# Another order of the three float32r products of a two-bank matmul group

## The chip, the cores and the metric

The kernel runs on one core of a Trainium2 chip. The metric is the time of one execution on the device in microseconds (us); three runs of the kernel before gave 841.36, 841.49 and 846.52, a median of 841.49. The profile is of one execution. Its engines are TensorE (PE for the matmuls, PEld for the loads of their weights), VectorE (DVE), ScalarE (ACT), GpSimd (POOL) and SyncE (SP, which issues most DMAs).

## The reference

One inference step of a two-layer decoder trunk, for 512 prompt rows and 8 sample rows (520 rows) of 1,024 channels, all in float32:

```python
# layer 0
z = x @ w_in                                   # 1024 -> 7 x 1024
a_val, a_gate, b_post, c_pre, h, g = split(z)  # g has 2 x 1024
a = silu(layer_norm(causal_conv31(a_val * sigmoid(a_gate))))
b = b_post * causal_conv3(c_pre * h)
x = layer_norm(alpha * x + (concat(a, b) * silu(g)) @ w_out)
# layer 1
z = x @ w_in_c                                 # 1024 -> 3 x 2048
u, v, g = split(z)
v = layer_norm(gelu(v))
y = gelu(u) * (tril(w_s) v + b_s) * silu(g)    # chunks of 128 positions, 8 heads
x = layer_norm(alpha * x + y @ w_out_c)
```

It returns the rows of both groups, the last rows of the conv inputs and the v rows of the sample group.

## The kernel before

**Tiling.** Channels lie on the 128 partitions and the 520 rows on the free dimension, so that x is 8 k tiles of 128 x 520. A weight *unit* is a block of 1,024 input channels by 128 output channels: 8 tiles (one for each k tile) of 128 x 128. One unit gives one output tile z of 128 x 520, which fills two PSUM banks with 260 rows each (`TH = 260`; `hs(h)` is the h-th half of the rows).

**Three products.** To keep float32's precision with float32r operands, both operands are split into a high and a low part. `load_unit` (L115 to L125) does so for the weights: SyncE's queue loads `raw`, ScalarE copies it to `whi` (L121), and VectorE or GpSimd subtracts to get `wlo` (L124; `ON_POOL` says which units are GpSimd's). The rows have parts named xh and xl, x1h and x1l, or yh and yl, of which the first is the high one. Each product is then hi x high + lo x high + hi x low, so that a unit takes 8 k tiles x 3 products x 2 halves = 48 matmuls of 128 x 128 weights and 260 columns.

**The three places that write such products.** `mm2` (L152 to L163, matmul at L157) does a whole unit into two banks; it serves the gate, val, c, h and post projections, both silu gates (z_gb, z_ga), the first half of each output projection (z_o, z_q), ten of the v units, and u and the gate of layer 1 (z_u, z_gc). `mm` (L136 to L146, matmul at L141) does one half of the rows into one bank; it serves the second halves of the output projections (z_p) and six of the v units. The first two units (z_first, matmul at L207) are done as their data arrives, in a loop of their own: within a k tile, for each of the three products, for each of the two units, both halves.

**Buffers.** The split weights rotate through 12 buffers, hi and lo in turn (some units use others), and `unit` asks for a unit five calls ahead (`LEAD = 5`). The `raw` buffers are three. The tiles z of two banks rotate through two, so that a call of mm2 may run while the tile before is read. VectorE and ScalarE read both halves of z in one instruction, but for the last gate of each branch (two silu steps, L415), z_o's third tile (two adds, L461) and the first units.

**Order.** The program is written in its logical order and a planner orders each engine's queue by a simulated timeline, with the order of writing as the priority. The wide conv of layer 0 (`acc`, L269, 30 multiply-adds of 128 x 512 for each of 8 channel tiles on VectorE) is marked as background work: it fills VectorE between the steps that the projections need, among them `apad` (L306), `ch` (L325), the short conv `sB` (L332) and the product with z_post (L392). `split_y` (L395 to L405) makes the high and low parts of the gated rows; `out_part` (L473) does the second half of an output projection with its layer norm.

Of the kernel before, what the change touches and what calls it, by code (L numbers as in the profile page):

```python
# [17 lines left out]
D = 1024  # L18
# [12 lines left out]
ALPHA = 4.0 ** 0.25  # L31
EPS = 1e-5

# columns of the packed per-channel parameters
PA_W = 0
PA_B = 31
PA_G = 32
# [13 lines left out]
def decoder_kernel(  # L51
# [30 lines left out]
    def xs_slot(dt, name):  # L82
        return slots.tile([P, T], dt, tag="X", name=name, bufs=16)
# [16 lines left out]
    def mt(name):  # L100
        return mps.tile([P, 512], F32, tag="m", name=name)
# [7 lines left out]
    def hs(h):  # L109
        return slice(h * TH, (h + 1) * TH)  # L110

# [1 line left out]
    n_units = 2 + wu.shape[0]  # L113
    units = [None, None]

# [16 lines left out]
    def unit(n):  # L132
        while len(units) < min(n + 1 + LEAD, n_units):
            load_unit(("M", 4) if len(units) in EXTRA else ("W", 12))
        return units[n]
# [16 lines left out]
    def mm2(z, w, ah, al):  # L152
        hi, lo = w
        for k in range(KT):
            for h in range(2):
                for j, (a, b) in enumerate(((hi, ah), (lo, ah), (hi, al))):
                    nc.tensor.matmul(  # L157
                        z[h][:, :TH],
                        a[:, k, :],
                        b[k][:, hs(h)],  # L160
                        start=(k == 0 and j == 0),
                        stop=(k == KT - 1 and j == 2),
                    )  # L163

    # products of a constant until the first rows are there, so that the array's clock is up by then
    warm = const.tile([P, P], BF16, name="warm")
    nc.vector.memset(warm, 1.0)
    wps = mt("warm")
    for j in range(NWARM):
        nc.tensor.matmul(wps[:, :P], warm, warm, start=True, stop=True)  # L170

    # the input rows come with the first two weight units, one k tile after the other, and the
    # products follow in that order
    xh, xl = [], []
    w0h, w0l = [], []
    zg = zt("z_first")
# [2 lines left out]
    for k in range(KT):  # L179
# [5 lines left out]
        q, j = k // 4, k % 4  # L185
        nc.sync.dma_start(raw[:, j], w0[:, k])
        cuts = 2 if k == 0 else 1
# [3 lines left out]
        h = xs_slot(F32R, f"xh_{k}")  # L191
        lo = xs_slot(F32R, f"xl_{k}")
# [22 lines left out]
    load_unit()  # L215
    pa = const.tile([P, KT, NPA], F32, name="pa")
    nc.sync.dma_start(pa, pa_in)
    # powers of two, so float32r holds them as well
    ones_r = const.tile([P, P], F32R, name="ones_r")
    ones_d = ones_r.bitcast(F32)  # L220
    nc.gpsimd.memset(ones_d, 1.0 / D)
# [6 lines left out]
    neg_half = const.tile([P, NS], F32, name="neg_half")  # L228
    nc.gpsimd.memset(neg_half, -0.5)

    # ================= layer 0 =================
    unit(1)
    xs = []
    for j in range(2):
        t = wpool.tile([P, 4, NS, WA], F32, tag="M", name=f"xs_{j}", bufs=4)
# [46 lines left out]
    n = 0  # L282
    for i in range(KT):
# [44 lines left out]
        s = slots.tile([P, T], F32, tag="SB", name=f"sB_{i}", bufs=8)  # L328
# [9 lines left out]
                op1=ALU.add,  # L338
            )

    # the sample rows of both convolutions
    nc.gpsimd.dma_start(cbs_out, xb)
    prodb = btmp("prodb")[:, : KT * NS * WB].rearrange("p (a b c) -> p a b c", a=KT, b=NS)
    nc.vector.tensor_tensor(
# [23 lines left out]
                    cA[i][:, SEQ:], cas[:, i - 4 * j, :], AF.Identity, bias=pa[:, i, PA_B : PA_B + 1]  # L368
                )

    # layer norm of the wide convolution over the channels, then silu
    def mean_of(m, src, name):
        """the sum of src / D over the channels, from its two float32r parts"""
        both = tpool.tile([P, T], F32R, tag="B", name=f"parts_{name}", bufs=4)
        nn = src.shape[-1]
        hi, lo = both[:, :nn], both[:, TH : TH + nn]
        nc.scalar.copy(hi, src)
        nc.vector.tensor_tensor(lo, src, hi.bitcast(F32), op=ALU.subtract)
        nc.tensor.matmul(m, ones_r, hi, start=True, stop=False)
        nc.tensor.matmul(m, ones_r, lo, start=False, stop=True)  # L380
# [11 lines left out]
        nc.vector.tensor_tensor(two(sB[i]), zh(z), two(sB[i]), op=ALU.mult)  # L392

    def split_y(i, g, other, tag, parts):
        """y = g * other as its two parts, in that many cuts of the rows"""  # L395
        h = y_slot(F32R, f"yh_{tag}{i}")
        lo = y_slot(F32R, f"yl_{tag}{i}")
        for j in range(parts):
            c = slice(j * T // parts, (j + 1) * T // parts)
            nc.vector.tensor_tensor(g[:, c], g[:, c], other[:, c], op=ALU.mult)  # L400
            nc.scalar.copy(h[:, c], g[:, c])
            nc.vector.tensor_tensor(lo[:, c], g[:, c], h[:, c].bitcast(F32), op=ALU.subtract)
        yh.append(h)
        yl.append(lo)
# [66 lines left out]
    gated(cA, "a")  # L471

    def out_part(base, c0, c1, yh, yl, res, lnc, done, last=False, pool_sub=()):  # L473
        """The second half of an output projection for the rows c0..c1, the residual, and the layer
        norm over the channels. The sums of the norm are of the rows less the mean of their first
        512 channels, so that no large mean cancels in the variance."""
        c = slice(c0, c1)
        nn = c1 - c0
        key = f"{base}_{c0}"
# [92 lines left out]
    def split_x1(d, c0, c1):  # L572
# [10 lines left out]
    out_part(n, TH, T, yh, yl, res, LN0_G, split_x1)()  # L583
    n += KT

    # ================= layer 1 =================
    wt = wpool.tile([P, NH, P], F32, tag="M", name="wt", bufs=4)
    nc.gpsimd.dma_start(wt, wsT_in)
    bs = wpool.tile([P, NH, P], F32, tag="M", name="bs", bufs=4)
    nc.gpsimd.dma_start(bs, bs_in)  # L590
    # wt[s, h, t] is kept where s <= t
    nc.gpsimd.affine_select(
        wt, wt, pattern=[[0, NH], [1, P]], compare_op=ALU.is_ge, fill=0.0, base=0, channel_multiplier=-1
    )
    # and its float32r parts, for the column sums
    wth, wtl = [], []
    for j in range(2):
        w = wt[:, 4 * j : 4 * j + 4, :].rearrange("p a b -> p (a b)")
# [29 lines left out]
    for i in range(NVF):  # L628
        z = one(i, f"z_v{i}_1")[:, :TH]
        mm(z, unit(n + i), x1h, x1l, hs(1))  # L630
        t = vt[i]
# [18 lines left out]
    def v_finish():  # L650
        v_tok(NV - 1)
        for c in range(NC):
            nc.vector.bn_aggr(mv[:, c, :], stats[:, c, :, :].rearrange("p a b -> p (a b)"))
        nc.vector.tensor_scalar_add(rs, mv[:, :, 1], EPS)
        nc.gpsimd.tensor_tensor(rs, rs, neg_half[:, :NC], op=ALU.pow)
        for i in range(NV):
            for c in range(NC):
                nc.vector.tensor_scalar(
                    vtok[i][:, c * P : (c + 1) * P],
                    vtok[i][:, c * P : (c + 1) * P],  # L660
                    mv[:, c, 0:1],
                    rs[:, c : c + 1],
                    op0=ALU.subtract,
                    op1=ALU.mult,
                )
        # column sums of the causal weights, for the shift of the norm
        for j in range(2):
            m = mt(f"rows_{j}")
            nc.tensor.matmul(m, ones_r, wth[j], start=True, stop=False)
            nc.tensor.matmul(m, ones_r, wtl[j], start=False, stop=True)  # L670
            nc.scalar.mul(
                rowsum[:, 4 * j : 4 * j + 4, :].rearrange("p a b -> p (a b)"), m, float(D)
            )
        # the sample rows' layer norm
        ssum = tiny.tile([P, NS], F32, name="ssum")
        nc.vector.tensor_reduce(ssum, vs.rearrange("p a b -> p b a"), axis=AX.X, op=ALU.add)
        m = mt("vs_mean")
        nc.tensor.matmul(m[:, :NS], ones_d, ssum, start=True, stop=True)
        smean = tiny.tile([P, NS], F32, name="smean")
        nc.vector.tensor_scalar_mul(smean, m[:, :NS], 0.5)  # L680
        bc = lambda t: t[:, None, :].to_broadcast([P, NV, NS])
        nc.vector.tensor_tensor(vs, vs, bc(smean), op=ALU.subtract)
        vq = mixs
        nc.vector.tensor_tensor(vq, vs, vs, op=ALU.mult)
        qsum = tiny.tile([P, NS], F32, name="qsum")
        nc.vector.tensor_reduce(qsum, vq.rearrange("p a b -> p b a"), axis=AX.X, op=ALU.add)
        m = mt("vs_var")
        nc.tensor.matmul(m[:, :NS], ones_d, qsum, start=True, stop=True)
        srs = tiny.tile([P, NS], F32, name="srs")
        nc.vector.tensor_scalar(srs, m[:, :NS], 0.5, EPS, op0=ALU.mult, op1=ALU.add)  # L690
        nc.gpsimd.tensor_tensor(srs, srs, neg_half, op=ALU.pow)
        nc.vector.tensor_tensor(vs, vs, bc(srs), op=ALU.mult)
        pb = lambda j: pv[:, :, j : j + 1].to_broadcast([P, NV, NS])
        nc.vector.tensor_tensor(vs, vs, pb(0), op=ALU.mult)
        nc.vector.tensor_tensor(vs, vs, pb(1), op=ALU.add)
        nc.gpsimd.dma_start(vs_out, vs)
        four = lambda t: t.rearrange("p (a c) b -> p a c b", c=2)
        nc.vector.tensor_tensor(
            four(mixs), four(vs), ws00[:, :, None, None].to_broadcast([P, NH, 2, NS]), op=ALU.mult
        )  # L700
        nc.vector.tensor_tensor(
            four(mixs), four(mixs), bs[:, :, None, 0:1].to_broadcast([P, NH, 2, NS]), op=ALU.add
        )
# [83 lines left out]


def _units(w, e0, e1):
    """[1024, e] columns e0..e1 as [n, 128 (k inside), 8 (k tile), 128]"""  # L790
    w = w[:, e0:e1]
    n = (e1 - e0) // P
    return w.reshape(KT, P, n, P).transpose(2, 1, 0, 3)


def _chan(a, n):
    """[..., n*128] -> [128, n, ...]"""
    a = a.reshape(a.shape[:-1] + (n, P))
    k = a.ndim
    return a.transpose((k - 1, k - 2) + tuple(range(k - 2)))  # L800
# [86 lines left out]
```

## Time and profile before

| what | value |
|---|---|
| runs, us | 841.36, 841.49, 846.52 (median 841.49) |
| the profiled execution: span, us | 840.8 (first to last instruction; the page has no other time of it) |
| matmuls and weight loads | 6,792 each |
| PE busy, us | 816.4 (97%) |
| DVE busy, us | 557.8 (66%) |
| ACT busy, us | 309.5 (37%) |
| POOL busy, us | 193.7 (23%) |
| mean granted TensorE clock | 0.991 |
| DMA moved | 82.38 MB, mean 98 GB/s |

A row of a timeline gives the start and the length in us, engine, line, operation, output and inputs by the program's names, shapes and a count. Matmuls are pipelined and the ends of their rows are modelled, so the pitch is read from start to start. A row of waits reads: engine, its tile and line, the engine, tile and line that it waited for, then us in total, times, and the longest. A row of the chain gives start, length and what ran. A row of stages gives the stage and its length, then for PE, PEld, DVE, ACT and POOL the busy us and the count, then the granted clock, the busy share of the DMA engines and GB/s.

### The profile page before, as it was taken

Reading aid. Unit: us, or ns where it says so; the run is one execution under the profiler, and the core shown is the slowest. Engines: PE = TensorE matmul, PEld = TensorE weight load, DVE = VectorE, ACT = ScalarE, POOL = GpSimd, SP = SyncE. Lnnn points to the kernel's source line nnn. Section 1 sums busy time; section 2 is a strip of 40 time slices with the busy share of each in tenths; the row PEclk is TensorE's granted clock in tenths of the full one; section 3 lists DMA queues with packets and bytes.
Section 4 is the critical chain, followed back from the end, with each engine's and each line's share of the span. In section 5 each row is a group of like instructions: output and inputs, shape, how many; then the busy total and the mean of one; then the engine's idle time right before and its main releaser. Section 6 shows DMA issues by size and latency. Waiting matters only on the chain.

```text
span 840.8 us, 15982 instructions
## 1 busy us (share of the span) xinstructions
PE 816.4 (97%) x6792; PEld 813.8 (97%) x6792; DVE 557.8 (66%) x894; ACT 309.5 (37%) x470; POOL 193.7 (23%) x178
## 2 busy tenths in 40 slices
PE   9989999998999999999999999999999999999994
PEld 8989999998999999999999999999999999999993
DVE  5899999999994487356696333495455433625566
ACT  5423322333124346333466533333432133333243
POOL 0844355544340000024252711101000000000022
PEclk9999999999999999999999999999999999999998
DMA  8533333223223452424050522204223233222011
GB/s 301 164 103 101 101 103 102 96 82 130 72 79 101 122 166 66 126 76 126 26 166 12 171 81 82 95 24 156 77 76 95 82 101 94 83 79 99 1 51 51
DMA packets 27110, 82.38 MB, mean 98 GB/s; under 512 B 3568, under 2 KB 7296, under 8 KB 27040
## 3 DMA queue, kind: packets, MB, share of 16 engines
q1 hardware_dynamic: 26000, 79.01, 30.1%
q0 software_dynamic: 1040, 2.36, 0.7%
q8 instruction: 53, 0.87, 0.4%
q14 instruction: 17, 0.14, 0.1%
HBM read 77.91 MB, written 3.44 MB: 97 GB/s over the span
## 4 chain that ended last, share of the span: by engine, by line
PE 71%; DVE 23%; DMA 2%; issue 2%; ACT 1%; SPq 0%; POOL 0%; ACTq 0%; DVEq 0%; POOLq 0%
DVE acc L269 14%; PE z_gc L157 11%; PE z_u L157 11%; PE z_p L141 9%; PE z_v L157 7%; PE z_q L157 5%; PE z_o L157 5%; PE z_gb L157 5%; PE z_ga L157 5%; PE z_post L157 4%; PE z_v L141 4%; DVE sB L332 3%; DMA raw<-in_wu 2%; PE mix L713 2%; PE vt L615 1%
## 5 line engine op out<-in xcount | busy, mean ns | idle before, releaser
L121 ACT CAST whi<-raw 128x1024 fp32r<-128x1024 f32 x134 | 140.0, 1047 | 300.6 <-issue 66.6
L124 POOL TENSOR_TENSOR wlo<-raw,whi 128x1024 fp32r<-128x1024 f32 x60 | 145.6, 2434 | 262.6 <-ACT whi L121 262.3
L124 DVE TENSOR_TENSOR wlo<-raw,whi 128x1024 fp32r<-128x1024 f32 x74 | 90.2, 1222 | 131.0 <-ACT whi L121 131.0
L269 DVE SCALAR_TENSOR_TENSOR acc<-apad,pa,acc 128x512 f32<-128x512 f32 x240 | 166.6, 748 | 2.5 <-ACT acc L266 0.8
L157 PE MATMUL z_gc<-x1h,whi 128*128 128x260 f32 x256 | 72.9, 285 | 0.0
L157 PE MATMUL z_u<-x1h,whi 128*128 128x260 f32 x256 | 72.4, 283 | 0.0
L157 PE MATMUL z_gc<-x1h,wlo 128*128 128x260 f32 x256 | 72.0, 281 | 0.0
L157 PE MATMUL z_u<-x1l,whi 128*128 128x260 f32 x256 | 72.0, 281 | 0.0
L157 PE MATMUL z_gc<-x1l,whi 128*128 128x260 f32 x256 | 72.0, 281 | 0.0
L157 PE MATMUL z_u<-x1h,wlo 128*128 128x260 f32 x256 | 72.0, 281 | 0.0
L157 PEld LDWEIGHTS z_u<-x1h,wlo 128*128 128x128 f32 x256 | 48.1, 188 | 0.1
L157 PEld LDWEIGHTS z_gc<-x1h,wlo 128*128 128x128 f32 x256 | 48.2, 188 | 0.0
L157 PEld LDWEIGHTS z_u<-x1h,whi 128*128 128x128 f32 x256 | 48.1, 188 | 0.1
L157 PEld LDWEIGHTS z_gc<-x1l,whi 128*128 128x128 f32 x256 | 48.1, 188 | 0.0
L157 PEld LDWEIGHTS z_u<-x1l,whi 128*128 128x128 f32 x256 | 48.1, 188 | 0.0
L157 PEld LDWEIGHTS z_gc<-x1h,whi 128*128 128x128 f32 x256 | 48.1, 188 | 0.0
L725 POOL COPY mix<-mixs 128x8 f32<-128x8 f32 x16 | 3.5, 226 | 186.5 <-DVE gu L752 174.1
L157 PE MATMUL z_v<-x1h,whi 128*128 128x260 f32 x160 | 46.0, 287 | 0.0
L157 PE MATMUL z_v<-x1h,wlo 128*128 128x260 f32 x160 | 45.0, 281 | 0.0
L157 PE MATMUL z_v<-x1l,whi 128*128 128x260 f32 x160 | 44.9, 281 | 0.0
L157 PE MATMUL z_post<-xh,whi 128*128 128x260 f32 x128 | 36.8, 288 | 4.2 <-DVE sB L392 4.2
L157 PE MATMUL z_h<-xh,whi 128*128 128x260 f32 x128 | 36.9, 288 | 4.0 <-DVE apad L306 4.0
(259 smaller groups left out, 2758.5 us busy)
## 6 DMA issues: line engine op xcount, KB each, us to landing
raw<-in_wu SPq DMA_DIRECT2D x134, 512.0 KB, 3.6
xr<-in_xT SPq DMA_DIRECT2D x8, 260.0 KB, 4.6
x<-in_xT SPq DMA_DIRECT2D x7, 260.0 KB, 4.4
out_y<-r SPq DMA_DIRECT2D x8, 130.0 KB, 1.8
out_y<-out SPq DMA_DIRECT2D x4, 260.0 KB, 2.2
raw_s<-in_w SPq DMA_DIRECT2D x8, 128.0 KB, 4.2
xs<-in_cache_a SPq DMA_DIRECT2D x2, 496.0 KB, 9.2
out_cas<-xs POOLq DMA_DIRECT2D x2, 496.0 KB, 4.5
```

The lines of the kernel that those rows point to most:

```text
L121: nc.scalar.copy(hi, raw)
L124: eng.tensor_tensor(lo, raw, hi.bitcast(F32), op=ALU.subtract)
L141: nc.tensor.matmul(ps, a[:, k, :], b[k][:, c], start=(k == 0 and j == 0), stop=(k == KT - 1 and j == 2),)
L157: nc.tensor.matmul(z[h][:, :TH], a[:, k, :], b[k][:, hs(h)], start=(k == 0 and j == 0), stop=(k == KT - 1 and j == 2),)
L269: nc.vector.scalar_tensor_tensor(acc[i], apads[i][:, j : j + SEQ], pa[:, i, PA_W + j : PA_W + j + 1], acc[i], op0=ALU.mult, op1=ALU.add,)
L332: nc.vector.scalar_tensor_tensor(s[:, :SEQ], ch[:, j : j + SEQ], pa[:, i, PB_W + j : PB_W + j + 1], s[:, :SEQ], op0=ALU.mult, op1=ALU.add,)
L615: nc.tensor.transpose(m[:, c * P : (c + 1) * P], vt[i][:, c * P : (c + 1) * P], ident)
L713: nc.tensor.matmul(m[:, c * P : (c + 1) * P], vtok[i][:, c * P : (c + 1) * P], wt[:, h, :], start=True, stop=True)
L725: nc.gpsimd.tensor_copy(t[:, SEQ:], mixs[:, i, :])
```

## The change

Inside a k tile of `mm2` the loop over the three products is now outside and the loop over the two halves inside, and the products come in the order hi x high, hi x low, lo x high. Before, the order of a k tile was hi, lo, hi into the first bank and hi, lo, hi into the second. After, it is hi, hi, hi, hi, lo, lo, with the bank changing at every matmul. The same 48 matmuls are written, with the same operands and the same start and stop marks on each bank's first and last. `mm` and the loop at L207 stay as they are; the other changed lines are comments.

```diff
     def mm2(z, w, ah, al):
         hi, lo = w
         for k in range(KT):
-            for h in range(2):
-                for j, (a, b) in enumerate(((hi, ah), (lo, ah), (hi, al))):
+            for j, (a, b) in enumerate(((hi, ah), (hi, al), (lo, ah))):
+                for h in range(2):
                     nc.tensor.matmul(
                         z[h][:, :TH],
                         a[:, k, :],
                         b[k][:, hs(h)],
...
                         stop=(k == KT - 1 and j == 2),
                     )
```

## The prediction

> **What bounds the kernel now.** I read the page's totals and slices first, then the stages, then what TensorE waits for, then the chain that ended last.
>
> ```profile
> PE 816.4 (97%) x6792; PEld 813.8 (97%) x6792; DVE 557.8 (66%) x894; ACT 309.5 (37%) x470; POOL 193.7 (23%) x178
> PE   9989999998999999999999999999999999999994
> DVE  5899999999994487356696333495455433625566
> PEclk9999999999999999999999999999999999999998
> ```
>
> TensorE is busy from end to end, and VectorE is full beside it only in slices 3 to 12. There is one weight load (PEld) for each matmul, 6,792 of both, so the program leaves out no load, whatever stands in the array. The stages (length, then each engine's busy us and count, then the granted clock and the DMA):
>
> ```profile
> 8.00:17.70 9.70, 9.70 (x83) 9.70 (x82) 7.20 (x14) 6.35 (x12) 0.00 (x0) 1.00 1.01 360
> 17.70:212.00 194.30, 185.25 (x1539) 184.44 (x1537) 188.95 (x248) 64.30 (x91) 98.89 (x71) 0.99 0.36 113
> 212.00:385.70 173.70, 173.70 (x1448) 173.70 (x1449) 112.99 (x138) 67.15 (x92) 25.46 (x11) 0.99 0.33 102
> 472.40:779.00 306.60, 306.60 (x2580) 306.43 (x2579) 144.20 (x269) 100.84 (x130) 18.90 (x32) 1.00 0.29 91
> ```
>
> From 17.7 to 212 us VectorE works 188.95 of 194.30 us and TensorE is the one that waits (9.05 us idle). From 212 us on TensorE has no idle time in the two long stages, and VectorE has a third to a half to spare. All that TensorE waited for in the whole span:
>
> ```profile
> PE z_post L157 <- DVE sB L392: 4.2, 1, 4.2
> PE z_h L157 <- DVE apad L306: 4.0, 1, 4.0
> PE warm L170 <- DVE warm L167: 1.1, 1, 1.1
> PE shift L497 <- DVE tot L492: 0.8, 1, 0.8
> PE z_p L141 <- DVE yl_a L402: 0.8, 1, 0.8
> PE z_gate L157 <- ACT c L317: 0.6, 1, 0.6
> PE z_first L207 <- ACT xh L200: 0.6, 1, 0.6
> PE z_c L157 <- DVE wlo L124: 0.2, 1, 0.2
> ```
>
> Two of these are long, and both are waits for a late VectorE. The chain agrees: up to 211.98 us it runs mainly through VectorE's conv steps, and from there through matmuls in long unbroken pieces:
>
> ```profile
> 211.98 35.84 PE z_post L157 x288
> 247.81 45.65 PE z_gb L157 x384
> 402.37 12.01 PE z_p L141 x100
> 634.87 45.97 PE z_q L157 x384
> ```
>
> So the pitch of the matmuls sets the time after 212 us: 45.65 / 384 = 118.9 ns in z_gb, 45.97 / 384 = 119.7 ns in z_q. Both come out of mm2 (L157), with the same shape and loop; only the operands' places differ. The change touches mm2 alone: 112 calls of 48 matmuls, 5,376 of the 6,792. mm2 runs in 32 calls before 212 us (all 32 of the gate, val, c and h projections bar the two written at L207, and two of z_post: 30 + 2), and in 80 calls, 3,840 matmuls, after it.
>
> **The change part by part.** It adds and removes no instruction. It moves matmuls inside groups of six. Of the five seams inside a group and the one to the next group, before has four where the weights change and the bank stays, one where the weights stay and the bank changes (between the halves), and one where both change (to the next k tile). After, the weights stay and the bank changes at four, and both change at two. Both seams of the new order are therefore in the old trace. Here is z_c's first k tile (start, length, engine); its first half is hi, lo, hi up to 18.43, its second starts at 18.55:
>
> ```profile
> 18.43 0.28 PE L157 MATMUL z_c<-xl,whi 128*128 128x260 f32 x1
> 18.43 0.19 PEld L157 LDWEIGHTS z_c<-xh,whi 128*128 128x128 f32 x1
> 18.55 0.28 PE L157 MATMUL z_c<-xh,whi 128*128 128x260 f32 x1
> 18.67 0.28 PE L157 MATMUL z_c<-xh,wlo 128*128 128x260 f32 x1
> 18.79 0.28 PE L157 MATMUL z_c<-xl,whi 128*128 128x260 f32 x1
> 18.91 0.28 PE L157 MATMUL z_c<-xh,whi 128*128 128x260 f32 x1
> ```
>
> From 18.43 to 18.55 the same whi k tile serves again and the bank changes; there is still a load of 0.19 us, and the step is 0.12 us. From 18.55 to 18.67 and to 18.79 the weights change and the bank stays: 0.12 us each. From 18.79 to 18.91 both change: 0.12 us. At this resolution the order has no price. One place already runs nearly the new order for a long time: the products at L207 use each weight tile twice in a row and change the bank with every matmul.
>
> ```profile
> L207 PEld LDWEIGHTS z_first<-xh,whi_s x32: 186/188/334, 4.1 to 16.5; 128*128 128x128 f32 x32
> L207 PE MATMUL z_first<-xh,whi_s x32: 278/283/584, 4.1 to 16.6; 128*128 128x260 f32 x32
> ```
>
> The loads number 32 for 32 matmuls there too, though 16 of them repeat the tile before. In time, four matmuls to a row:
>
> ```profile
> 9.11 0.64 PE L207 MATMUL z_first<-xh,whi_s 128*128 128x260 f32 x4
> 17.23 0.65 PE L207 MATMUL z_first<-xl,whi_s 128*128 128x260 f32 x4
> ```
>
> From 9.11 to 17.23 us lie 17 such rows, 68 matmuls, so the pitch is 8.12 / 68 = 119.4 ns.
>
> *Pitch.* The nearest row, L207, is 0.5 ns above z_gb; z_q, in the old order, is 0.8 ns above z_gb. A difference of 0.5 ns is thus what another place of the operands makes, and I take 0 for the order, with 0.8 ns to either side as its bounds: nothing in the rows excludes a small gain. VectorE hides it up to 212 us. After that it is 3,840 x 0.8 ns = 3.1 us either way. If VectorE's cover in the first stage were gone, the other 1,536 matmuls would add 1.2 us.
>
> *The low part is needed later.* wlo is read by the fifth matmul of a call and no longer by the second. Only one call waited for it, z_c at 17.71 us:
>
> ```profile
> 17.71 0.28 PE L157 MATMUL z_c<-xh,whi 128*128 128x260 f32 x1
> 18.20 0.39 PE L157 MATMUL z_c<-xh,wlo 128*128 128x260 f32 x1 [0.20 <-DVE wlo L124]
> ```
>
> The step is 0.49 us where 0.12 is usual, a loss of 0.37, and three matmuls now stand in between (0.36 us), which covers it. VectorE leads from there to 212 us, so I count 0.2 us of the 0.37 as gained (bounds 0 and 0.4).
>
> *The second half's rows are needed sooner.* The first products of z_o and z_q read the rows that were just split. The high rows of half 1 are read two matmuls earlier (0.24 us); z_o and z_q do not appear among the waits above. I count 0, or 0.24 us at each if there were no slack.
>
> *The weight buffers come free at another time.* The last reader of a whi was the last matmul of a call and is now the third from the end, 0.24 us sooner; the last reader of a wlo was the second from the end and is now the last, 0.12 us later. The next whi copy waits on ScalarE for just that event:
>
> ```profile
> ACT whi L121 <- PE z_u L157: 44.9, 14, 4.7
> ```
>
> ```profile
> L121 ACT CAST whi<-raw 128x1024 fp32r<-128x1024 f32 x134 | 140.0, 1047 | 300.6 <-issue 66.6
> ```
>
> The copy, the read of z that is queued behind it on ScalarE, the lo subtraction that follows it on GpSimd or VectorE and the next raw load on SP's queue may all start up to 0.24 us sooner. The lo buffer is not short: its subtraction comes after a copy of 1.05 us (this group's mean). TensorE waits for no weights after z_c's 0.2 us, so this is worth 0: the units are asked for five calls ahead, and without that lead a call would gain or lose the 0.12 to 0.24 us.
>
> *The banks.* The first half's bank is finished one matmul before the end and no longer three (0.24 us later). Nearly all reads take both halves in one instruction and wait for the last matmul, whose time does not move. The exceptions are the last gate of each branch and z_o's third tile. After z_ga's last call TensorE waits 0.8 us for yl_a; I charge 0 with 0.24 us as the bound.
>
> The sum: 841.5 us (median; the profiled span is 840.8, so 0.7 lies around it) - 0.2 + 0 = 841.3 us. The bounds of the small terms give 841.5 - 0.4 - 3.1 = 838.0 and 841.5 + 3.1 + 0.24 x 3 = 845.3.
>
> **The rivals.**
>
> *The repeated weights are not loaded again, chance 0.03.* Then a matmul could follow at the speed of its 260 columns. The clock's half-speed stretch shows that speed, since there the load has twice the time to hide:
>
> ```profile
> 51.60 0.42 PE L157 MATMUL z_h<-xh,whi 128*128 128x260 f32 x1
> 52.90 0.42 PE L157 MATMUL z_h<-xh,whi 128*128 128x260 f32 x1
> ```
>
> Six matmuls in 1.30 us are 216.7 ns, 108.3 at full clock, 10.6 under the 118.9. At four seams in six this saves 3,840 x 4/6 x 10.6 ns = 27 us, and the time is 814; with the first stage too it is 803. Against it stand the loads at L207 and in z_c's fence, present for a tile that was already there. The Trainium skill ("TensorE: Matmul & The Clock Gate", step 1 of Step-by-step: what each phase is for) says that weights can be loaded once and used by several matmuls, since the load is an instruction of its own. The trace does not agree for this kernel: a load goes with each matmul.
>
> *The bank's change lets the clock fall, chance 0.01.* If TensorE paused at each change of bank, the clock could drop; at half clock a matmul takes 97.8 ns more, 376 us over 3,840. The L207 stage changes the bank every time and has clock 1.00 in the stage row 8.00:17.70. The Trainium skill (the same page, A second HAM failure mode: psum-queue depth-cycling) tells of a kernel that cycled through banks, idled for moments and lost its clock again and again. The trace does not agree so far.
>
> *VectorE's waits in the first stage come or go.* At 36 us this happens (VectorE, then GpSimd; below it a stage row):
>
> ```profile
> 35.72 0.74 DVE L269 SCALAR_TENSOR_TENSOR acc<-apad,pa,acc 128x512 f32<-128x512 f32 x1
> 36.37 7.68 DVE L332 SCALAR_TENSOR_TENSOR sB<-ch,pa,sB 128x512 f32<-128x512 f32 x1
> 36.37 7.13 POOL L124 TENSOR_TENSOR wlo<-raw,whi 128x1024 fp32r<-128x1024 f32 x3
> ```
>
> ```profile
> 50.90:54.40 3.50, 3.49 (x16) 3.49 (x17) 3.46 (x6) 2.14 (x3) 3.46 (x4) 0.53 0.02 4
> ```
>
> An sB step whose operands are all in SBUF lasts 7.68 us while GpSimd runs three lo subtractions, where an acc step of that size takes 0.74; TensorE then waits 4.0 us for apad and runs 3.5 us at clock 0.53, in which it does 16 matmuls and not 29, another 1.6 us. One such event is worth 5.6 us. The planner that orders VectorE's and GpSimd's queues sees the earlier and later release of the buffers, and may place steps otherwise; so a lo subtraction that starts before such an sB step makes one more event, and one that starts after it removes one. For: the two start at the same hundredth, and the moves of 0.12 to 0.24 us are of the size that decides. Against: in that place GpSimd's start follows from its own queue, which the change doesn't touch, and the background steps leave VectorE little freedom. One long wait gone: 835.7 us, chance 0.12. Both gone: 830, chance 0.05. **Slower than before:** one more event 846.9, chance 0.12; it decides as soon as one more sB step meets a lo subtraction for over the 5.7 us that two z buffers cover (a call is 48 x 118.9 ns). Two or more: 852.5 and up, chance 0.10.
>
> **How the numbers follow.** The forecast, 841.3 us with 838.0 to 845.3 of its own, has chance 0.57. Faster by over 1% (under 833.1) takes both waits gone and the spared loads: 0.08. Slower by over 1% (over 849.9) takes two or more events and the clock: 0.11. The rest, 0.81, is within 1%, about what a measurement of this kernel can tell from no change (the runs before lie 0.6% apart). The range reaches from one wait gone less some of the pitch bound, 834, to one more event plus the pitch bound, 849, and leaves out 0.19.
>
> **What would show it.** PEld x6792 again; z_gb x384 at 45.3 to 46.0 us in the chain; z_q no further from z_gb than 0.8 ns; no wait of z_c for wlo. The forecast is wrong if PEld falls under 6,792, if a pitch of L157 leaves 118 to 121 ns, if the clock drops in a stage after 215 us, or if the list of TensorE's waits loses z_h or z_post or gains another of some 4 us. In the first three the seams were misread, in the last the order of VectorE's queue decided.

## The result and the profile after

The changed kernel took 839.27 us (median of 5 runs, 836.90 to 840.34). The kernel before, with two more runs, had a median of 843.58 us. The ratio is 0.9946 with a 95% interval of 0.9922 to 0.997: 0.5% faster, a difference that is there, but below the 1% that the chances went by. The profiled execution has a span of 835.9 us (840.8 before), 1.7 below its own time of 837.64.

The page's totals and three of its rows of slices, after:

```profile
PE 816.1 (98%) x6792; PEld 813.3 (97%) x6792; DVE 552.9 (66%) x894; ACT 309.6 (37%) x470; POOL 194.8 (23%) x178
...
PE   9989899999999999999999999999999999999994
...
DVE  5999999999984486446795332596355433525566
...
PEclk9999999999999999999999999999999999999998
```

There are 6,792 weight loads again, so nothing was spared there. VectorE is busy 4.9 us less, although its instructions are the same 894. What TensorE waited for, after (us in total, times, longest):

```profile
PE z_gate L157 <- ACT c L317: 2.6, 1, 2.6
PE z_h L157 <- DVE apad L306: 2.3, 1, 2.3
...
PE shift L497 <- DVE tot L492: 0.8, 1, 0.8
PE z_p L141 <- DVE yl_a L402: 0.7, 1, 0.7
PE z_post L157 <- DVE sB L392: 0.2, 1, 0.2
```

The wait for z_post has shrunk from 4.2 to 0.2 us, that for z_h from 4.0 to 2.3; that for z_gate grew from 0.6 to 2.6; z_c's for wlo is gone. The same stages as before, each cut within a few matmuls of the same place (stage and its length, then PE, PEld, DVE, ACT and POOL busy, granted clock, DMA share, GB/s):

```profile
17.70:207.20 189.50, 184.41 (x1534) 183.57 (x1533) 184.79 (x247) 63.44 (x91) 99.13 (x70) 1.00 0.38 114
207.20:381.00 173.80, 173.80 (x1452) 173.80 (x1453) 112.47 (x138) 68.30 (x94) 26.70 (x11) 1.00 0.35 104
467.10:774.00 306.90, 306.90 (x2577) 306.73 (x2576) 144.21 (x269) 100.38 (x129) 18.93 (x32) 1.00 0.31 91
```

The first stage gained most: 189.5 us where 194.3 were needed. The rows of the later two say little on the pitch, since their counts differ by up to four matmuls (1,452 for 1,448, some 0.5 us). Part of the gain lies just behind the first stage. Before, TensorE ran at half clock after its wait of 4.2 us for z_post, 13 matmuls in 2.93 us:

```profile
211.97:214.90 2.93, 2.92 (x13) 2.92 (x14) 2.93 (x3) 0.00 (x0) 1.75 (x1) 0.50 0.02 8
```

After, the stage that begins at this point has a clock of 1.00. In all eleven profiles of this document, every wait of TensorE of 4.0 us or more was followed by such a stretch; of the waits of 1.7 to 2.6 us some were, and some were not. The chain's pieces of matmuls, after:

```profile
207.16 34.76 PE z_post L157 x288
241.91 45.98 PE z_gb L157 x384
629.89 46.20 PE z_q L157 x384
```

z_post starts 211.98 - 207.16 = 4.8 us sooner and its 288 matmuls take 34.76 us for 35.84, so that z_gb starts 247.81 - 241.91 = 5.9 us sooner. The program ends 4.9 us sooner, so 1.0 us is given back on the way. The pitch shows where: 45.98 / 384 = 119.7 ns for 118.9 in z_gb, and 46.20 / 384 = 120.3 for 119.7 in z_q. In these calls the new order makes TensorE *slower*, and the kernel became faster all the same. Two questions follow: what took the z_post wait away, and what raised the pitch.

### The profile page after: what moved, and what is told of

Its sections match the earlier page's. It is cut to its first block, busy times and chain, and to the rows that moved or that the text cites. A ratio compares the mean times of both kernels' runs of the same rounds, so it can differ in the third digit from the quotient of the medians.

```text
span 835.9 us, 15971 instructions
## 1 busy us (share of the span) xinstructions
PE 816.1 (98%) x6792; PEld 813.3 (97%) x6792; DVE 552.9 (66%) x894; ACT 309.6 (37%) x470; POOL 194.8 (23%) x178
## 4 chain that ended last, share of the span: by engine, by line
PE 82%; DVE 13%; issue 1%; ACT 1%; ACTq 0%; DVEq 0%
PE z_gc L157 11%; PE z_u L157 11%; PE z_p L141 9%; PE z_v L157 7%; DVE acc L269 6%; PE z_q L157 6%; PE z_gb L157 5%; PE z_o L157 5%; PE z_ga L157 5%; PE z_post L157 4%; PE z_v L141 4%; PE z_gate L157 3%; PE z_h L157 3%; PE z_c L157 3%; PE z_val L157 3%; DVE sB L332 2%
## 5 line engine op out<-in xcount | busy, mean ns | idle before, releaser
L157 PE MATMUL z_gc<-x1h,whi 128*128 128x260 f32 x256 | 51.9, 284 | 0.0
L157 PE MATMUL z_u<-x1h,whi 128*128 128x260 f32 x256 | 51.6, 282 | 0.0
L157 PE MATMUL z_gc<-x1h,wlo 128*128 128x260 f32 x256 | 51.6, 283 | 0.0
L157 PE MATMUL z_u<-x1h,wlo 128*128 128x260 f32 x256 | 51.6, 282 | 0.0
L157 PE MATMUL z_gc<-x1l,whi 128*128 128x260 f32 x256 | 51.4, 282 | 0.0
L141 PE MATMUL z_p<-yl_a,whi 128*128 128x260 f32 x128 | 36.2, 284 | 0.7 <-DVE yl_a L402 0.7
L141 PE MATMUL z_p<-yh_c,whi 128*128 128x260 f32 x128 | 36.2, 284 | 0.0
L141 PE MATMUL z_p<-yh_a,wlo 128*128 128x260 f32 x128 | 36.2, 284 | 0.0
L141 PE MATMUL z_p<-yh_c,wlo 128*128 128x260 f32 x128 | 36.1, 283 | 0.0
L141 PE MATMUL z_p<-yh_a,whi 128*128 128x260 f32 x128 | 36.0, 282 | 0.0
```

Of the source, the lines that this page charges most:

```text
L141: nc.tensor.matmul(ps, a[:, k, :], b[k][:, c], start=(k == 0 and j == 0), stop=(k == KT - 1 and j == 2),)
L157: nc.tensor.matmul(z[h][:, :TH], a[:, k, :], b[k][:, hs(h)], start=(k == 0 and j == 0), stop=(k == KT - 1 and j == 2),)
```

## The experiments

Theory Q: the planner did write part of VectorE's and ScalarE's queues otherwise. Near 205 us the changed kernel has acc_7's first step ahead of sB_7's, and a few later swaps; GpSimd's and SyncE's queues are the same. That swap could have freed z_post. Theory M: the queues do not matter, and it is the meetings that decide. A meeting is an sB step of VectorE that overlaps a lo subtraction (wlo) of GpSimd; the prediction showed one at 36 us. Each ratio below is to the kernel before, run beside it.

**Both kernels once more.** No edit.

> The kernel before, profiled a second time, to see which of its waits come back. Theory Q (the planner's order of VectorE's queue near 205 us decides): ratio 1.000 within 0.003, TensorE waits about 4 us for z_post again, since the queue is the same. Theory M (chance meetings of GpSimd's lo subtractions with VectorE's sB steps decide): ratio also near 1.000, but the wait for z_post need not be there: anything from 0 to 4 us, and sB steps of over 2 us at other places than in the first profile. Pitch in z_gb 118.9 ns in both.

> The changed kernel, profiled a second time. Theory Q: ratio 0.9946 within 0.003, TensorE's wait for z_post again under 0.5 us. Theory M: the same ratio within 0.005, but the wait for z_post may be anything from 0 to 4 us, and the long sB steps stand at other places. Pitch in z_gb 119.7 ns in both, as in the first profile of the changed kernel.

The kernel before came to a ratio of 0.9993 (0.9973 to 1.0013), the changed one to 0.996 (0.9945 to 0.9974). TensorE's waits, before again:

```profile
PE z_post L157 <- DVE sB L392: 4.2, 1, 4.2
PE z_h L157 <- DVE apad L306: 2.3, 1, 2.3
...
PE z_gate L157 <- ACT c L317: 0.6, 1, 0.6
PE z_c L157 <- DVE wlo L124: 0.5, 1, 0.5
```

And after again:

```profile
PE z_h L157 <- DVE apad L306: 1.8, 1, 1.8
...
PE z_gate L157 <- ACT c L317: 0.4, 1, 0.4
...
PE z_post L157 <- DVE sB L392: 0.2, 1, 0.2
```

The waits for z_h and z_gate differ between two profiles of one kernel, so no difference in them can be put down to the change. The wait for z_post is 4.2 us in both profiles of the one kernel and 0.2 in both of the other. In one point theory M missed: the long sB steps of the kernel before did not move to other places but came again at the same ones, 1.7 us sooner (2.86 us at 157.62, then 2.86 at 155.94). A profile is of one execution, and single executions of the two kernels overlap (836.91 to 844.80 us before again, 837.71 to 841.04 after again), so the meetings of the others are not known.

**The two halves of the change.** First the products' order alone, and second the loops alone:

```diff
-                for j, (a, b) in enumerate(((hi, ah), (lo, ah), (hi, al))):
+                for j, (a, b) in enumerate(((hi, ah), (hi, al), (lo, ah))):
```

```diff
-            for h in range(2):
-                for j, (a, b) in enumerate(((hi, ah), (lo, ah), (hi, al))):
+            for j, (a, b) in enumerate(((hi, ah), (lo, ah), (hi, al))):
+                for h in range(2):
```

> Half of the change: the halves stay outside, the products come as hi x high, hi x low, lo x high, so the bank changes twice a k tile as before. The planner's queues of VectorE, ScalarE, GpSimd and SyncE are then word for word those of before. Theory Q: ratio 1.000 within 0.003 and the wait for z_post is about 4 us. Theory M: the release of the weight buffers moves by 0.12 us, so the ratio may be anywhere from 0.993 to 1.003. If the bank's change with every matmul is what raised the pitch, z_gb is at 118.9 ns; if it is the products' order, at 119.7.

> The other half of the change: the halves inside, the products in their old order hi x high, lo x high, hi x low. The planner's queues are those of the changed kernel up to 212 us. Theory Q: ratio 0.995 within 0.003, wait for z_post under 0.5 us. Theory M: anything from 0.993 to 1.003. Pitch in z_gb 119.7 ns if the bank's change raised it, 118.9 if the products' order did.

The products alone gave 0.9968 (0.9946 to 0.9989), the loops alone 0.9972 (0.9958 to 0.9986). With the products alone, the list of waits and the chain have:

```profile
PE z_post L157 <- DVE sB L392: 0.3, 1, 0.3
```

```profile
241.06 46.24 PE z_gb L157 x384
```

Here all queues are those of before, and the z_post wait is down to 0.3 us nevertheless: the new queue is not needed for that. The pitch is 46.24 / 384 = 120.4 ns although the bank changes no more often than before. With the loops alone z_gb takes 46.09 us, 120.0 ns, and the wait is 0.2 us. Neither of the two values expected, 118.9 and 119.7, came. Either half raises the pitch in z_gb, so the bank's change is not needed for it. Nor does it always raise it: with the loops alone, where the bank changes with every matmul, z_q takes 45.87 us, less than the 45.97 of before.

**The queue alone.** The matmuls keep their old order, and the planner is told to queue sB_7's first step behind acc_7's:

```diff
-        nc.scalar.mul(s[:, :SEQ], ch[:, 0:SEQ], pa[:, i, PB_W : PB_W + 1])
+        with tc.issue_after(first[7]) if i == 7 else ExitStack(): nc.scalar.mul(s[:, :SEQ], ch[:, 0:SEQ], pa[:, i, PB_W : PB_W + 1])
```

> The kernel before with the planner made to put acc_7's first step ahead of sB_7's on ScalarE, as in the changed kernel; VectorE's queue near 205 us is then that of the changed kernel but for one acc step. The matmuls keep their old order. Theory Q (the queue decides): the wait for z_post under 0.5 us and ratio 0.995 within 0.003. Theory M: sB steps of over 2 us near 157 and 180 us as before, the wait for z_post 3.5 to 4.5 us, ratio 1.000 within 0.003.

Measured: 1.0004 (0.9983 to 1.0025), and the two long waits are

```profile
PE z_post L157 <- DVE sB L392: 4.3, 1, 4.3
PE z_h L157 <- DVE apad L306: 4.2, 1, 4.2
```

Theory Q falls from both sides: the old queue without the wait, the new queue with it.

**The addresses alone.** Each x tile of 520 columns lies in a buffer of 528; instructions, their order and all queues are those of before:

```diff
-        return slots.tile([P, T], dt, tag="X", name=name, bufs=16)
+        return slots.tile([P, 528], dt, tag="X", name=name, bufs=16)[:, :T]
```

> The kernel before with each x tile of 520 columns in a buffer of 528, so that the x tiles and all that lies behind them have other addresses; queues and instructions are those of before. If the pitch hangs on where the operands lie, z_gb's differs from 118.9 ns by 0.3 or more; if it hangs on the order of the products and banks alone, it is 118.9 again. Theory M besides: a pitch that is 0.4 ns or more higher moves the meetings as in the changed kernel, and the wait for z_post falls under 1 us; with 118.9 it stays near 4.

Measured: 0.9969 (0.9952 to 0.9987). The chain has

```profile
242.41 46.08 PE z_gb L157 x384
632.69 45.97 PE z_q L157 x384
```

z_gb, which reads x tiles, rises to 46.08 / 384 = 120.0 ns; z_q, which reads y tiles, stays at 119.7. So the pitch moves by 1.1 ns with the operands' places and with no other order. The z_post wait is 0.3 us here. In these runs a slower pitch in z_gb, however it was made, goes with a faster kernel.

**Where it is decided.** In the kernel before, VectorE and then GpSimd near 157 us:

```profile
157.62 2.86 DVE L332 SCALAR_TENSOR_TENSOR sB<-ch,pa,sB 128x512 f32<-128x512 f32 x1
...
157.51 2.43 POOL L124 TENSOR_TENSOR wlo<-raw,whi 128x1024 fp32r<-128x1024 f32 x1 [2.68 <-ACT whi L121]
```

and in the changed kernel:

```profile
156.18 0.75 DVE L332 SCALAR_TENSOR_TENSOR sB<-ch,pa,sB 128x512 f32<-128x512 f32 x1
...
156.25 2.97 POOL L124 TENSOR_TENSOR wlo<-raw,whi 128x1024 fp32r<-128x1024 f32 x1 [2.73 <-ACT whi L121]
```

Before, the lo subtraction starts 0.11 us ahead of the sB step, which then lasts 2.86 us. After, the sB step is 0.07 us ahead and lasts 0.75, and the subtraction is the one drawn out, to 2.97 us. The Trainium skill ("SBUF — State Buffer", Who interferes with whom) says that a VectorE instruction with two SBUF inputs contends with a GpSimd instruction that reads SBUF, that one with a single SBUF input does not (outside VectorE's two-port modes), and that the order of issue decides who is blocked. These rows agree, 2.86 against 0.75 us by who comes first; and no acc step, which has one SBUF input, lasted over 0.76 us in any profile here.

Why the 0.18 us? The meeting before this one is four calls of mm2 earlier, and in both kernels GpSimd starts first there:

```profile
134.69 2.41 POOL L124 TENSOR_TENSOR wlo<-raw,whi 128x1024 fp32r<-128x1024 f32 x1 [2.03 <-ACT whi L121]
```

```profile
133.27 2.40 POOL L124 TENSOR_TENSOR wlo<-raw,whi 128x1024 fp32r<-128x1024 f32 x1 [2.05 <-ACT whi L121]
```

From there VectorE is full, and its way to the next sB step is a fixed list of work. GpSimd's next start hangs on TensorE, which releases the weight buffer at the end of a call: before, z_gate's call ends at 156.25 us, ScalarE's whi copy starts at 156.38 and the subtraction behind it at 157.51. From lo start to lo start it is 157.51 - 134.69 = 22.82 us before, which is 4 x 48 x 118.9 ns, and 156.25 - 133.27 = 22.98 us after, 4 x 48 x 119.7 ns. The slower matmuls bring the subtraction 0.16 us later, and VectorE slips in ahead. All nine profiles with the sum in SBUF, by this meeting ("lo to lo" is from the lo start of the meeting before):

| kernel | z_gb pitch, ns | lo to lo, us | sB start less lo start, us | sB step, us | wait for z_post, us |
|---|---|---|---|---|---|
| before | 118.9 | 22.82 | +0.11 | 2.86 | 4.2 |
| before again | 118.9 | 22.82 | +0.11 | 2.86 | 4.2 |
| new queue | 118.9 | 22.83 | +0.10 | 2.87 | 4.3 |
| lo subtractions later (below) | 118.9 | 22.82 | +0.08 | 2.90 | 4.4 |
| after | 119.7 | 22.98 | -0.07 | 0.75 | 0.2 |
| after again | 119.7 | 22.98 | -0.08 | 0.74 | 0.2 |
| products alone | 120.4 | 23.11 | -0.19 | 0.75 | 0.3 |
| loops alone | 120.0 | 22.87 | +0.04 | 0.74 | 0.2 |
| x padded | 120.0 | 23.04 | -0.14 | 0.75 | 0.3 |

In all nine the sB step starts 22.90 to 22.93 us after the lo start of the meeting before, whatever the kernel. So the length of four calls decides who is first. The loops alone fit this: their z_gb has 120.0 ns, but the four calls of this place only 119.2 (192 matmuls from 131.79 to 154.67 us), and the margin stays at +0.04 us. VectorE was not held up there, and it was at +0.08; what decides between these two is not shown.

With the time saved there VectorE loses less at the next meeting too (the two sB steps near 180 us take 0.75 and 2.30 us before, 1.01 and 0.74 after), and it reaches z_post in time. From the sB step ahead of this meeting to z_post's start it is 56.3 to 56.5 us in the four profiles with the long wait, and 52.6 to 53.4 in the other five. For the first comparison that is 56.34 - 52.96 = 3.4 us of the 4.8 by which z_post starts sooner. The other 1.4 us were there already (155.64 against 154.20 us); that part differs between profiles of one kernel, as the wait for z_h does, and is 0.9 us in the two repeats.

**The lo subtractions later.** A copy of 8 columns (its result is not used) stands ahead of each lo subtraction of units 4 to 45 on GpSimd:

```diff
-        eng = nc.gpsimd if n in ON_POOL else nc.vector
+        eng = nc.gpsimd if n in ON_POOL else nc.vector; n in range(4, 46) and nc.gpsimd.tensor_copy(late, hi.bitcast(F32)[:, 0, :8])
```

> The kernel before with a copy of 8 columns of whi put on GpSimd ahead of each lo subtraction of units 4 to 45 (its result is not used), so that these subtractions start about 0.2 us later; matmuls, addresses of the operands and all other queues stay, but for one swap on VectorE near 205 us. Theory M (at 157 us an sB step lost to a subtraction that began 0.1 us sooner; what came after follows from the time lost there): the sB steps near 157 and 180 us are back at 0.75 us or so, the wait for z_post falls from 4.2 to under 1 us at a pitch of 118.9 ns in z_gb, and the ratio is 0.990 to 0.997. Rival (the slower matmuls themselves remove the wait, since VectorE has more time for each call): with the pitch of before the wait stays at 3.5 to 4.5 us and the ratio at 1.000 within 0.003.

Measured: 0.9999 (0.9987 to 1.0012), with a wait for z_post of 4.4 us; my numbers for theory M missed and the rival's came. VectorE, then GpSimd:

```profile
155.71 2.90 DVE L332 SCALAR_TENSOR_TENSOR sB<-ch,pa,sB 128x512 f32<-128x512 f32 x1
...
155.48 0.19 POOL L123 COPY late<-whi 128x8 f32<-128x8 f32 x1 [2.53 <-ACT whi L121]
155.63 2.42 POOL L124 TENSOR_TENSOR wlo<-raw,whi 128x1024 fp32r<-128x1024 f32 x1
```

The subtraction does start later in its call, but so does the sB step, and the margin is 0.08 us for 0.11. VectorE was held up by the subtraction at 132.81 us too, and set out from its end: a constant delay of GpSimd shifts both sides of the next meeting. Only something that changes the time *between* two meetings shifts one against the other, and the calls' length does. So M's claim that any shift of GpSimd will do is wrong. Nor do the early meetings count: the sB steps near 64 and 86 us are short in this run (0.75 and 0.74 us), and the wait for z_post is there.

The rival's number came, but its reason is too small. In the changed kernel the slower matmuls give VectorE some 1,536 x 0.86 ns = 1.3 us more before z_post, and the wait fell by 4.0. No run moves the meeting at 157 us alone; that it is the one rests on the nine profiles and on the next two runs.

**The meetings taken away.** The running sum of the short conv goes to PSUM, so that an sB step has one input in SBUF as an acc step has. Nothing is left out, and all queues keep their order:

```diff
-        nc.scalar.mul(s[:, :SEQ], ch[:, 0:SEQ], pa[:, i, PB_W : PB_W + 1])
+        sp = mt(f"sp_{i}"); nc.scalar.mul(sp, ch[:, 0:SEQ], pa[:, i, PB_W : PB_W + 1])
         for j in range(1, WB):
             nc.vector.scalar_tensor_tensor(
-                s[:, :SEQ],
+                sp if j < WB - 1 else s[:, :SEQ],
                 ch[:, j : j + SEQ],
                 pa[:, i, PB_W + j : PB_W + j + 1],
-                s[:, :SEQ],
+                sp,
```

> The kernel before with the short conv's running sum in PSUM instead of SBUF, so that an sB step has one SBUF operand like an acc step, of which none was drawn out in any trace. All queues are word for word those of before; nothing is left out. Theory M (the meetings of sB steps with GpSimd's lo subtractions cost the waits): all sB steps near 0.75 us, the waits for z_h and z_post gone or under 0.5 us, 11 us less with the clock they cost, ratio 0.987 within 0.003. Rival (VectorE is too slow in that stage anyway): the sB steps are short, but the waits stay at 2 us or more each and the ratio is above 0.994.

> The same with the changed kernel. Theory M: what the change won was only the meetings, and its own effect is a pitch of 0.2 to 0.8 ns more, so with the meetings taken from both it is slower than the kernel before with the sum in PSUM by 1.5 to 2.7 us (0.2 to 0.3%): ratio to the kernel before 0.989 to 0.990. Rival (the new order helps TensorE itself): it stays ahead of it by 0.4 to 0.5%, ratio 0.982 or so.

With the old order of the matmuls: 832.4 us (831.76 to 832.77), ratio 0.9877 (0.9857 to 0.9897). With the new one: 833.4 us (833.18 to 833.57), ratio 0.989 (0.9873 to 0.9907). The sB steps of the first (shortest, median and longest ns):

```profile
L332 DVE SCALAR_TENSOR_TENSOR sp<-ch,pa,sp x8: 742/751/757, 32.1 to 192.1; 128x512 f32<-128x512 f32 x8
L332 DVE SCALAR_TENSOR_TENSOR sB<-ch,pa,sp x8: 733/743/746, 33.4 to 194.9; 128x512 f32<-128x512 f32 x8
```

None is over 0.76 us, where one of before lasted 7.68. The first is 10.6 us under the 842.97 of the kernel before beside it, for 11 expected. In the list of TensorE's waits z_h is gone and z_post stands at

```profile
PE z_post L157 <- DVE sB L392: 0.3, 1, 0.3
```

Without meetings the changed order is 1.0 us slower than the old one, and the runs of the two do not overlap. I had expected 1.5 to 2.7. The chain of the first has the old pitch,

```profile
235.96 45.65 PE z_gb L157 x384
...
670.89 22.85 PE z_u L157 x192
```

and that of the second the new one:

```profile
236.13 45.98 PE z_gb L157 x384
...
671.61 22.90 PE z_u L157 x192
```

A call that reads x tiles pays 0.33 / 8 = 0.04 us for the new order, one of z_u (x1 tiles) only 0.05 / 4 = 0.01; I had reckoned nearer the first for all. The kernel before with this sum in PSUM is the fastest version here, 0.8% under the changed kernel of the first comparison (832.4 for 839.27).

## Why the prediction was right, and where not

The forecast was no change within 1%, 841.3 us and a range of 834 to 849. Measured were 839.27 us and 0.5% less than before, so the time and the class hold. That the time came so near is in part luck: the sum had neither of the two effects that made the difference, a wait of 4.0 us that went and 1.0 us of pitch that came. And the kernel before itself, with two more runs, stands at 843.58 and not at the 841.49 that the sum began with.

*Loads and clock.* Right. PEld stayed at 6,792, and the clock did not fall with the bank's change (1.00 in the three stages after). The two rivals with the spared loads and the falling clock did not come. The price of the first was not well founded: in the half-speed stretch the rows of the loads last longer too, 0.33 us for 0.19, so 108.3 ns is not shown to be the speed of a matmul without a load.

*Pitch.* This term of the sum was mis-sized. "I take 0 for the order, with 0.8 ns to either side as its bounds": z_gb rose by 0.86 ns, from 118.9 to 119.7, a little over the bound, z_q by 0.6, z_u by 0.1 to 0.3. The rows of z_c's fence, given to 0.01 us, could not show a step of that size. That the operands' places alone move the pitch by as much was right, and the padded tiles showed it. The bill from z_gb on was 1.0 us, inside the 3.1 of the bound.

*"VectorE hides it up to 212 us."* Right that it costs nothing there, wrong that it does nothing there. The slower calls moved GpSimd against VectorE by 0.16 us over four calls, and by all that the runs show that removed 4.0 us of waiting and the half clock behind it.

*The waits of the first stage.* The rival named the mechanism, its price (5.6 us for an event) and the direction in which it could go, and gave one wait gone a chance of 0.12. One went, which the prediction itself had named as a sign that its forecast is wrong. The time fell by 4.3 us (medians) or 4.9 (profiles) and not by 5.6; 1.0 us of that is the pitch. But I named the wrong cause, the earlier release of the weight buffers and the planner ("in the last the order of VectorE's queue decided"): with the padded tiles neither changes, and the wait went as well. And I looked at the wrong meeting, that at 36 us, which is there after the change too (7.68 us). The planner did place steps otherwise; its swap near 205 us, tried alone, had no effect that could be measured.

*wlo later.* Not contradicted: z_c's wait is in both lists of before (0.2 and 0.5 us) and in those of the loops alone and the padded tiles (0.6 and 0.4), and in neither of the changed kernel. But three kernels with the old order (the new queue, the later lo subtractions, the sum in PSUM) do not have it either, so the 0.2 us of the sum are not shown.

*z_ga and z_p.* Right: the wait for yl_a is 0.7 us after for 0.8 before.

## What to carry to other kernels

Two engines that hold each other up make a stage whose length hangs on hundredths of a microsecond; an edit elsewhere moved it here by 0.3 to 0.5%, in its repeat as well, although the gain was not the edit's own. Before crediting a reordering, take the contention away (here by moving one operand to PSUM) and compare again: the order of the matmuls turned out to cost 0.1%, and the contention 1.2%. Where each matmul brings its own weight load, as here, putting equal weights one behind the other spares nothing.

## What was not expected of the hardware

The pitch of these float32r matmuls of 260 columns depends on which operands follow each other and where they lie: 118.9, 119.7, 120.0 and 120.4 ns in z_gb for kernels with the same matmuls, and the same value in both profiles of each of the two that were repeated. What causes it stays open. The order is not needed, since padding alone raised it; and an order that raises it in z_gb can leave it or lower it elsewhere (the loops alone lowered z_q from 45.97 to 45.87 us). A VectorE step can wait through more than one GpSimd instruction: near 36 us an sB step lasted 7.7 to 7.9 us behind three lo subtractions of 2.4 us in seven of the nine profiles, and 5.3 us behind two in the other two (the halves of the change), where the third was drawn out to 2.8 us instead.
